# A streaming encoder step: one pool per tile tag, latent attention's tags laid anew, and reciprocal roots on ACT

## The chip, the cores and the metric

The kernel runs on one core of one Trainium2 chip. The metric is the device time of one execution in microseconds (us); of several runs the median counts.

## What is computed

Two layers of a hybrid encoder step, on a prompt of 512 rows (4 tiles of 128) and a sample of 8 streams with 16 new rows each and 1024 cached ones. All data are float32. Cut to what matters:

```
p = x @ w_in                     # columns for three branches
u = gelu(a_u);  v = layer_norm(gelu(a_v))          # per group of 64 columns
y_a = u * (w_s @ v + b_s)                          # branch A, chunked gMLP
q = rms(b_cq, g_cq) @ w_uq;  ckv = rms(b_ckv, g_ckv);  krope = rope(b_kr)
y_b = softmax(q_lat @ ckv.T + q_rope @ krope.T) @ ckv @ w_uv    # branch B, latent attention
y_c = stick_breaking(c_q, c_k, c_v)                # branch C
y = [rms(y_a) | rms(y_b) | rms(y_c)] * g_mix
x = layer_norm(ALPHA * x + y @ w_out)              # ln1
x = layer_norm(ALPHA * x + relu(x @ w_up + b_up)**2 @ w_down + b_down)   # ln2
rms(x) = x * rsqrt(mean(x*x) + EPS) * g;  layer_norm(x) = (x - mu) * rsqrt(var + EPS) * g + b
```

The normalised latents, keys and values of both lanes are outputs too.

## The kernel before

A float32 operand is split into a rounded part and a rest (`split`: a CAST on ACT, a subtraction on DVE or GpSimd, called POOL in the profile), and a product is three matmuls of these (`mm3`). Two lanes, prompt P and sample S, are written as generators and woven. Each layer runs in stages: `in` projects x (`xin` holds the transposed x, 32 KB a partition for the prompt and 8 KB for the sample), `mix` does the gMLP branch (`gm_group`, called for two prompt tiles at a time and for the sample rows), the stick-breaking of the prompt (`lane_psb`), and `latents`, whose results go to DRAM (`cqd`, `ckd`) and come back transposed; `mla` is the prompt's latent attention (`lane_pmla`), and `out` and `mlp` follow. The S lane works through the caches on the other side of the memory in the meantime.

Memory is a stack on each side. A stage opens a `pool_of`, whose tiles are told apart by tag, and closes it when it is done. After everything is written out, a planner (`Plan.schedule`, with a cost for every operation) sets the order of the instructions on each engine, and `follow` pins it. Its rule on memory and that of the framework are the same: a tile of a pool waits until all tiles of every closed pool whose region overlaps its own pool are done with. So a stage's first tile waits for the last one of the stage below it, wherever in the region it lies. Weights come through rings of raw buffers, `rawP` and `rawS` with three slots each, then as `w` (four slots); all DMAs are issued from the SP queue in the planned order.

Nearly every instruction is issued by one helper and so has line L417; DMAs have L433. Groups are therefore told apart by tile names: `gst` are the gMLP branch's sums and roots, `gvt` its gated values, `gh` their split form, `wsT` the spatial weights, `rs` the root of a norm, `mv` the mean and variance, `ss` a sum of squares, `wq`/`wuT` weights of latent attention, `cT`, `cN`, `kr` the split cached keys, values and rope keys, `sC`, `acc` and `x` banks of PSUM.

The root of a norm is made on POOL in two instructions, a multiply and add and a power of -0.5 (`rstd_of`), 70 times: 20 for `layer_norm`, 50 for `rms_to` and the latents. `gm_group` does the same six times on 128x4 or 128x8 numbers, and divides its mean on POOL too.

Of the kernel before, what the change touches and what calls it, by code (L numbers as in the profile page):

```python
# [11 lines left out]
F32 = mybir.dt.float32  # L12
# [3 lines left out]
ALU = mybir.AluOpType  # L16
# [482 lines left out]
def hybrid_step(  # L499
# [25 lines left out]
    def little(shape, dtype, tag):  # L525
        return sm.tile(shape, dtype, tag=tag + now["by"], name=tag, bufs=3 if now["by"] == "P" else 2)
# [20 lines left out]
    mhalf = cp.tile([128, 4, 4], F32, name="mhalf")  # L547
    dve.memset(mhalf, -0.5)
# [19 lines left out]

    class pool_of:


        def __init__(self, name, side=None):
            self.cm, self.side = tc.tile_pool(name=name, bufs=1, reuse_waits="tile", side=side), side

        def __enter__(self):
            self.slots = Slots(self.cm.__enter__(), pace, self.side)
            return self.slots

        def __exit__(self, *a):
            pace.plan.close_pool(self.slots.plan)  # L580
            return self.cm.__exit__(*a)
# [28 lines left out]

    def rstd_of(ss, k, n):
        t = little([128, 4], F32, "rs1")
        pool.tensor_scalar(t[:, :n], ss, k, EPS, ALU.mult, ALU.add)
        r = little([128, 4], F32, "rs2")
        pool.tensor_tensor(r[:, :n], t[:, :n], mhalf[:, 0, :n], ALU.pow)
        return r
# [112 lines left out]
    def gm_group(l, t0, nt, ws, gmx, gvt, pl, tag):  # L729
# [15 lines left out]
        pool.tensor_scalar(mu, mu, 1.0 / 64, 0.0, ALU.mult, ALU.add)  # L745
        dve.tensor_tensor(gv, gv, across(mu), ALU.subtract)
# [3 lines left out]
        pool.tensor_scalar(var, var, 1.0 / 64, EPS, ALU.mult, ALU.add)  # L750
        r = stat()
        pool.tensor_tensor(r, var, mhalf[:, :nt], ALU.pow)
# [271 lines left out]
    def lane_pmla(l):  # L1024
        mq_cm = pool_of(f"pmlb{l}", "left")
        mq = mq_cm.__enter__()
        mp_cm = pool_of(f"pmla{l}", "left")
        mp = mp_cm.__enter__()
# [195 lines left out]
        mq_cm.__exit__(None, None, None)  # L1224

    def lane_psb(l, zt, tt, yt_):
# [56 lines left out]
        def values(u):  # L1283
# [6 lines left out]
            for g in range(ng):  # L1290
                h = h0 + g
                for i in range(qt + 1):
                    b = slice((g * (qt + 1) + i) * 128, (g * (qt + 1) + i + 1) * 128)
                    pe.matmul(py[:, h * 128:(h + 1) * 128], wT[:, 0, b], vS[:, i, h].rearrange("p a d -> p (a d)"), start=(i == 0), stop=False)
                    pe.matmul(py[:, h * 128:h * 128 + 64], wT[:, 1, b], vS[:, i, h, 0], start=False, stop=(i == qt))
# [588 lines left out]
```

## Time and profile before

| | |
|---|---|
| three runs | 1797.98, 1798.75 and 1805.46 us, median 1798.75 |
| the profiled execution | 1802.48 us, of which the span of the trace is 1800.6 |
| busy over the span | PE 1689.7 (94%), DVE 1179.1 (65%), ACT 994.7 (55%), POOL 560.7 (31%) |
| mean granted clock of TensorE | 0.972 |
| DMA | 305.05 MB, 169 GB/s from and to HBM |

PE is TensorE's matmul, PEld its weight load. In a row of the timeline, the first number is the start in us from the span's start, the second the time until the group's end; the brackets give the idle time of the engine just before, and the instruction whose end released it. A clock of 1.00 is 2.4 GHz and 0.50 is 1.2 GHz.

### The profile page before, as it was taken

To read this page: it belongs to the slowest core of one execution; us is meant where nothing else is said; L and a number is where in the kernel's file an instruction comes from. 1 tells how busy PE (TensorE), PEld (TensorE's weight loads), DVE (VectorE), ACT (ScalarE), POOL (GpSimd) and SP (SyncE) were. 2 spreads that over 40 slices of the span, in tenths; PEclk is the share of its full clock that TensorE was granted. 3 is DMA by queue.
4 is the path that set the end of the run, shared out by engine and by line. 5 is a ranking of instruction groups with operands and counts; after the bars stand their busy time and mean duration, and the time that the engine had idled before them with its cause. 6 is when DMAs were issued, how large, how long until landed. Compare 5 with 4: busy or idle time off the path is not lost. (4 is left out here: it accounts for less than half of the span.)

```text
span 1800.6 us, 24422 instructions
## 1 busy us (share of the span) xinstructions
PE 1689.7 (94%) x8756; PEld 1421.8 (79%) x8756; DVE 1179.1 (65%) x1592; ACT 994.7 (55%) x1739; POOL 560.7 (31%) x478
## 2 busy tenths in 40 slices
PE   8997989899999999999899979899999989999998
PEld 6897878777877777888688968787877777788886
DVE  3575675865677577676726756858456774776666
ACT  4574684545665556463226737855457555564631
POOL 0122365743575300000101323666445643000001
PEclk9997999999999999999999979999999999999999
DMA  7225557346544688674442245663555355786732
GB/s 261 78 81 155 172 170 217 117 147 201 164 137 146 173 279 278 187 254 128 149 142 74 91 135 173 178 229 122 160 184 155 116 161 172 255 269 191 255 127 92
DMA packets 145817, 305.05 MB, mean 169 GB/s; under 512 B 32032, under 2 KB 46496, under 8 KB 145696
## 3 DMA queue, kind: packets, MB, share of 16 engines
q1 hardware_dynamic: 145696, 303.49, 53.1%
q8 instruction: 69, 1.13, 0.3%
q14 instruction: 52, 0.43, 0.1%
HBM read 286.14 MB, written 17.30 MB: 169 GB/s over the span
## 5 line engine op out<-in xcount | busy, mean ns | idle before, releaser
L417 PE MATMUL acc<-w,hT 128*128 128x512 f32 x1536 | 398.6, 397 | 3.0 <-DVE hT L417 1.4
L417 PE MATMUL acc<-yT,wx 128*128 128x512 f32 (+1 forms) x1632 | 400.0, 389 | 1.4 <-DVE wx L417 1.1
L417 PEld LDWEIGHTS acc<-yT,wx 128*128 128x128 f32 x1632 | 294.4, 193 | 59.5 <-DVE wx L417 1.5
L417 PEld LDWEIGHTS acc<-w,hT 128*128 128x128 f32 x1536 | 282.1, 189 | 65.9 <-DVE hT L417 3.1
L417 POOL TENSOR_TENSOR cT<-rawK,cT 128x512 fp32r<-128x512 f32 x128 | 201.1, 1578 | 178.7 <-ACT cT L417 157.1
L417 POOL TENSOR_TENSOR cN<-rawV,cN 128x512 fp32r<-128x512 f32 x128 | 194.3, 1524 | 167.7 <-ACT cN L417 160.9
L417 DVE TENSOR_TENSOR w<-rawP,w 128x1024 fp32r<-128x1024 f32 (+4 forms) x122 | 152.7, 1256 | 128.9 <-ACT w L417 127.8
L417 DVE TENSOR_TENSOR wS<-rawS,wS 128x1024 fp32r<-128x1024 f32 x144 | 175.2, 1223 | 78.9 <-ACT wS L417 78.7
L417 ACT CAST wS<-rawS 128x1024 fp32r<-128x1024 f32 x144 | 151.2, 1051 | 134.9 <-PE x L417 52.2
L417 PE MATMUL acc<-w,xT 128*128 128x512 f32 (+3 forms) x960 | 189.2, 352 | 4.0 <-ACT ev L417 2.2
L417 POOL TENSOR_SCALAR rs<-mv 128x1 f32<-128x1 f32 x20 | 24.3, 1216 | 528.7 <-DVE mv L417 528.5
L417 ACT CAST w<-rawP 128x1024 fp32r<-128x1024 f32 (+4 forms) x122 | 121.9, 1004 | 117.5 <-DMA rawP<-in_w_down_dram 61.5
L417 PEld LDWEIGHTS acc<-w,xT 128*128 128x128 f32 x960 | 161.1, 195 | 20.2 <-ACT ev L417 2.4
L417 DVE TENSOR_TENSOR xy<-xy,acc 128x512 f32<-128x512 f32 x128 | 86.8, 683 | 79.4 <-PE acc L417 78.4
L417 ACT CAST cN<-rawV 128x512 fp32r<-128x512 f32 x128 | 78.5, 619 | 76.1 <-DMA rawV<-in_t_ckvv_dram 35.9
L417 PE MATMUL x<-cN,pTs 128*128 128x256 f32 x512 | 98.7, 297 | 9.2 <-ACT cN L417 3.3
L417 PEld LDWEIGHTS x<-cN,pTs 128*128 128x128 f32 x512 | 82.1, 194 | 31.0 <-ACT cN L417 10.2
L417 PE MATMUL x<-wS,htS 128*128 128x512 f32 x384 | 100.7, 397 | 3.4 <-ACT wS L417 2.9
L417 ACT CAST cT<-rawK 128x512 fp32r<-128x512 f32 x128 | 78.5, 619 | 45.3 <-PE sC L417 20.1
L417 PE MATMUL sC<-wS,x1TS 128*128 128x512 f32 x384 | 98.4, 394 | 0.7 <-ACT x1TS L417 0.7
L417 DVE TENSOR_TENSOR wx<-rawP,wx 128x1024 fp32r<-128x1024 f32 x68 | 90.6, 1332 | 12.1 <-ACT wx L417 11.6
L417 PEld LDWEIGHTS x<-wS,htS 128*128 128x128 f32 x384 | 72.1, 189 | 21.1 <-ACT wS L417 3.3
(276 smaller groups left out, 2772.6 us busy)
## 6 DMA issues: line engine op xcount, KB each, us to landing
rawP<-in_t_wup_dram SPq DMA_DIRECT2D x64, 512.0 KB, 4.0
rawP<-in_w_down_dram SPq DMA_DIRECT2D x64, 512.0 KB, 4.1
rawS<-in_w_up_dram SPq DMA_DIRECT2D x64, 512.0 KB, 4.7
rawS<-in_w_down_dram SPq DMA_DIRECT2D x64, 512.0 KB, 4.4
rawK<-in_t_ckv_dram SPq DMA_DIRECT2D x64, 256.0 KB, 3.2
rawV<-in_t_ckvv_dram SPq DMA_DIRECT2D x64, 256.0 KB, 3.0
rawK<-in_t_sbk_dram SPq DMA_DIRECT2D x64, 256.0 KB, 2.8
rawV<-in_t_sbv_dram SPq DMA_DIRECT2D x64, 256.0 KB, 3.0
```

The costliest lines, as they stand in the source:

```text
L417: r = f(out, *a, **k)
```

## The change

Four edits.

1. `pool_of` no longer opens one pool for a stage, but one for each tag, when the tag is first used or where `lay` names it. When a stage is over, its tags are popped from the top of the side's stack as far as the stages above them are over too. Planner and framework thus wait for the region of a tag and no longer for that of a stage.
2. `lane_pmla` has one `pool_of` instead of two, and lays the tags of the first half of its work ahead in a fixed order.
3. `root` makes x^-0.5 on ACT, as exp(-0.5 ln(k x + EPS)): an ACTIVATE with Ln, whose scale is k and whose bias is a tile `eps`, and one with Exp. It takes the place of the two POOL instructions in `rstd_of` (70 times) and in `gm_group` (6 times). In `gm_group`, the mean's division on POOL and the subtraction on DVE become one `scalar_tensor_tensor` on DVE.
4. In the value product of `lane_psb`, the second matmul takes the same 128 columns as the first (80 matmuls of 64 columns before).

```diff
@@ pool_of
-        def __init__(self, name, side=None):
-            self.cm, self.side = tc.tile_pool(name=name, bufs=1, reuse_waits="tile", side=side), side
+        def __init__(self, name, side):
+            self.name, self.side, self.tags, self.over = name, side, {}, False
         def __enter__(self):
-            self.slots = Slots(self.cm.__enter__(), pace, self.side)
-            return self.slots
+            return self
+        def lay(self, *tags):
+            for tag in tags:
+                cm = tc.tile_pool(name=f"{self.name}_{tag}", bufs=1, reuse_waits="tile", side=self.side)
+                self.tags[tag] = Slots(cm.__enter__(), pace, self.side)
+                stacks[self.side].append((self, cm, self.tags[tag]))
+        def tile(self, shape, dtype, tag=None, name=None, bufs=1):
+            tag = tag or name
+            if tag not in self.tags:
+                self.lay(tag)
+            return self.tags[tag].tile(shape, dtype, tag, name, bufs)
         def __exit__(self, *a):
-            pace.plan.close_pool(self.slots.plan)
-            return self.cm.__exit__(*a)
+            self.over = True
+            st = stacks[self.side]
+            while st and st[-1][0].over:
+                _, cm, slots = st.pop()
+                pace.plan.close_pool(slots.plan)
+                cm.__exit__(*a)
...
+    def root(out, x, k):
+        act.activation(out, x, AF.Ln, bias=eps, scale=k)
+        act.activation(out, out, AF.Exp, scale=-0.5)
     def rstd_of(ss, k, n):
-        t = little([128, 4], F32, "rs1")
-        pool.tensor_scalar(t[:, :n], ss, k, EPS, ALU.mult, ALU.add)
-        r = little([128, 4], F32, "rs2")
-        pool.tensor_tensor(r[:, :n], t[:, :n], mhalf[:, 0, :n], ALU.pow)
+        r = little([128, 4], F32, "rs")
+        root(r[:, :n], ss, k)
         return r
@@ gm_group
-        pool.tensor_scalar(mu, mu, 1.0 / 64, 0.0, ALU.mult, ALU.add)
-        dve.tensor_tensor(gv, gv, across(mu), ALU.subtract)
+        dve.scalar_tensor_tensor(gv, across(mu), -1.0 / 64, gv, ALU.mult, ALU.add)
...
-        pool.tensor_scalar(var, var, 1.0 / 64, EPS, ALU.mult, ALU.add)
         r = stat()
-        pool.tensor_tensor(r, var, mhalf[:, :nt], ALU.pow)
+        root(r, var, 1.0 / 64)
@@ lane_pmla
-        mq_cm = pool_of(f"pmlb{l}", "left")
-        mq = mq_cm.__enter__()
         mp_cm = pool_of(f"pmla{l}", "left")
-        mp = mp_cm.__enter__()
+        mp = mq = mp_cm.__enter__()
+        mp.lay("cqT", "ckT", "d2", "qr", "rp2", "krT", "qT", "qrT", "rope", "mask", "knT", "vM")
@@ lane_psb
-                    pe.matmul(py[:, h * 128:h * 128 + 64], wT[:, 1, b], vS[:, i, h, 0], start=False, stop=(i == qt))
+                    pe.matmul(py[:, h * 128:(h + 1) * 128], wT[:, 1, b], vS[:, i, h].rearrange("p a d -> p (a d)"), start=False, stop=(i == qt))
```

The planner turns the first two edits into another order. Three places show it.

The first is ACT at the end of `mix` in layer 0, up to the split of the last two prompt tiles of the gMLP branch (the second `gh`); `gt<-gvt` is the square ahead of the variance, `junk` the sums of squares of norms. Before:

```order
L417 ACTIVATE gt<-gvt 128x512
L417 CAST w_1647<-rawP 128x768
L417 ACTIVATE junk,ss<-gt 128x256 x2
L417 ACTIVATE junk,ss<-acc 128x384
L417 CAST wq_1691<-rawS 128x768
L417 ACTIVATE junk,ss<-acc 128x256
L417 CAST wq_1696<-rawS 128x384
L417 ACTIVATE junk,ss<-acc 128x256
L417 CAST wq_1754<-rawS 128x768
L417 CAST wq_1759<-rawS 128x384
L417 CAST gh<-gvt 128x512
```

Now:

```order
L417 ACTIVATE gt<-gvt 128x512
L417 CAST w_1742<-rawP 128x768
L417 CAST mask<-rawP 128x128
L417 ACTIVATE gst<-gst,eps 128x8
L417 ACTIVATE gst<-gst 128x8
L417 ACTIVATE junk,ss<-gt 128x256
L417 CAST wq_1899<-rawS 128x384
L417 ACTIVATE rs<-ss,eps 128x1
L417 ACTIVATE junk,ss<-gt 128x256
L417 ACTIVATE rs<-rs 128x1
L417 CAST gh<-gvt 128x512
```

The root of `gst` is now two ACTIVATEs of ACT itself, three of the four `wq` CASTs stand ahead of it (two of them above these rows), and one between it and `gh`.

The second is the SP queue at the same place, where `cqd<-ev` writes latents to DRAM and `rawS<-in_w_uq` loads the weights of `wq`. Before:

```order
L433 DMA rawP<-in_c_mask_dram 128x128
L433 DMA cqd<-ev 128x384
L433 DMA rawP<-in_w_uq_dram 128x2x384
L433 DMA rope<-in_c_rope_dram 128x2x64
L433 DMA cq_1679<-cqd 128x384
L433 DMA rawS<-in_w_uq_dram 128x2x384
L433 DMA rawS<-in_w_uq_dram 128x384
L433 DMA rawP<-in_w_uq_dram 128x384
L433 DMA rawS<-in_w_uq_dram 128x2x384
L433 DMA rawP<-in_t_wkv_dram 128x1024
L433 DMA rawS<-in_w_uq_dram 128x384
L433 DMA rawS<-in_t_wukT_dram 128x1024
```

Now:

```order
L433 DMA rawS<-in_w_uq_dram 128x2x384
L433 DMA rawS<-in_w_uq_dram 128x384
L433 DMA rawS<-in_w_uq_dram 128x2x384
L433 DMA rope<-in_c_rope_dram 128x2x64
L433 DMA cq_1798<-cqd 128x384
L433 DMA cqd<-ev 128x384
L433 DMA rawP<-in_c_mask_dram 128x128
L433 DMA rawP<-in_w_uq_dram 128x2x384
L433 DMA rawP<-in_w_uq_dram 128x384
L433 DMA rawS<-in_w_uq_dram 128x384
L433 DMA rawP<-in_t_wkv_dram 128x1024
L433 DMA rawP<-cqd 128x768
```

Three of the loads of `wq` now stand ahead of the rope table and the mask; the transposed latents come back (`rawP<-cqd`) within these rows, which in the order of before they do twelve rows further on.

The third is DVE at the border between layer 0 and layer 1: the last norm of the prompt (`bst`, `mv`, `xy`), the weights of the next projection (`w`), and the transposed x of the next layer (`xT`). Before:

```order
L417 TENSOR_TENSOR xy<-xy,acc 128x512
L417 TENSOR_TENSOR w_8392<-rawP,w_8392 128x1024
L417 BN_STATS bst<-xy 128x6
L417 TENSOR_TENSOR w_8397<-rawP,w_8397 128x1024
L417 BN_AGGR mv<-bst 128x2
L417 TENSOR_TENSOR w_8402<-rawP,w_8402 128x1024
L417 SCALAR_TENSOR_TENSOR xy<-xy,mv,gl 128x1024
L417 TENSOR_TENSOR w_8407<-rawP,w_8407 128x1024
L417 SCALAR_TENSOR_TENSOR xy<-xy,rs_8328,gl 128x1024
L417 TENSOR_TENSOR xT<-acc,xT 128x4x128 x6
```

Now:

```order
L417 TENSOR_TENSOR xy<-xy,acc 128x512
L417 TENSOR_TENSOR w_8727<-rawP,w_8727 128x1024
L417 BN_STATS bst<-xy 128x6
L417 TENSOR_TENSOR xT<-acc,xT 128x4x128
L417 BN_AGGR mv<-bst 128x2
L417 TENSOR_TENSOR xT<-acc,xT 128x4x128
L417 SCALAR_TENSOR_TENSOR xy<-xy,mv,gl 128x1024
L417 TENSOR_TENSOR xT<-acc,xT 128x4x128
L417 SCALAR_TENSOR_TENSOR xy<-xy,rs,gl 128x1024
L417 TENSOR_TENSOR xT<-acc,xT 128x4x128 x3
L417 TENSOR_TENSOR w_8732<-rawP,w_8732 128x1024
L417 TENSOR_TENSOR w_8737<-rawP,w_8737 128x1024
```

The `xT` subtractions moved from behind four weight splits and the norm to between the norm's steps, behind one weight split.

## Rows read from the trace of the kernel before

**Rows 1.** The page's busy time: us, share of the span, instructions.

```profile
span 1800.6 us, 24422 instructions
...
PE 1689.7 (94%) x8756; PEld 1421.8 (79%) x8756; DVE 1179.1 (65%) x1592; ACT 994.7 (55%) x1739; POOL 560.7 (31%) x478
```

**Rows 2.** Stretches: length; busy and count of PE, PEld, DVE, ACT, POOL; clock; DMA share, GB/s.

```profile
136.00:180.00 44.00, 33.13 (x185) 31.83 (x184) 24.68 (x59) 19.14 (x49) 13.49 (x26) 0.77 0.50 155
...
256.00:276.00 20.00, 15.95 (x86) 12.49 (x86) 14.82 (x20) 14.81 (x31) 19.14 (x19) 0.83 0.69 165
...
880.00:910.00 30.00, 20.31 (x93) 16.60 (x91) 20.41 (x26) 8.07 (x13) 5.28 (x6) 0.83 0.53 160
...
1022.00:1080.00 58.00, 44.59 (x272) 42.01 (x271) 33.99 (x73) 23.59 (x58) 18.25 (x32) 0.82 0.45 137
```

**Rows 3.** The same view, of the stretches at the half clock.

```profile
142.00:152.24 10.24, 7.02 (x30) 7.02 (x31) 7.34 (x17) 3.25 (x7) 2.31 (x6) 0.50 0.34 113
...
169.31:179.55 10.24, 10.24 (x51) 10.24 (x51) 4.47 (x11) 4.23 (x9) 0.00 (x0) 0.50 0.26 72
...
892.94:903.18 10.24, 5.15 (x18) 4.59 (x19) 7.85 (x10) 4.56 (x8) 1.88 (x2) 0.50 0.80 204
...
1036.30:1049.95 13.65, 5.80 (x23) 5.62 (x24) 8.78 (x20) 4.14 (x10) 4.58 (x9) 0.50 0.36 123
...
1070.43:1077.26 6.83, 6.83 (x34) 6.83 (x33) 3.23 (x8) 2.35 (x6) 1.58 (x3) 0.50 0.43 145
```

**Rows 4.** Timeline, end of mix in layer 0, by engine; brackets: idle before, its releaser.

```profile
135.43 0.68 DVE L417 TENSOR_REDUCE gst<-gt 128x8 f32<-128x512 f32 x1
...
142.19 0.68 DVE L417 TENSOR_TENSOR gvt<-gvt,gst 128x512 f32<-128x512 f32 x1
...
139.43 1.65 POOL L417 TENSOR_TENSOR gst<-gst,mhalf 128x8 f32<-128x8 f32 x1
...
144.14 0.51 ACT L417 CAST wq<-rawS 128x384 fp32r<-128x384 f32 x1 [2.86 <-DMA rawS<-in_w_uq_dram]
144.56 0.61 ACT L417 CAST gh<-gvt 128x512 fp32r<-128x512 f32 x1
...
145.22 0.47 PE L417 MATMUL sC<-gh,wsT 128*128 128x128 f32 x1 [8.52 <-ACT gh L417]
```

**Rows 5.** Timeline of PE at the same place in layer 1.

```profile
1043.28 0.47 PE L417 MATMUL sC<-gh,wsT 128*128 128x128 f32 x1 [9.25 <-ACT gh L417]
```

**Rows 6.** Timeline at the border of the layers: ACT, DVE, PE.

```profile
893.88 1.04 ACT L417 CAST w<-rawP 128x1024 fp32r<-128x1024 f32 x1 [4.48 <-DMA rawP<-in_t_win_dram]
...
897.29 1.88 DVE L417 TENSOR_TENSOR xT<-acc,xT 128x512 fp32r<-128x512 f32 x3
...
898.03 2.18 PE L417 MATMUL acc<-identr,xy 128*128 128x128 f32 x9 [8.09 <-DVE xT L417]
```

**Rows 7.** Groups by shape: busy us, mean ns | idle before, releasers.

```profile
L417 POOL TENSOR_TENSOR rs<-rs,mhalf 128x1 f32<-128x1 f32 x70 | 46.6, 669 | 4.9 <-POOL rs L417 0.2
...
L417 POOL TENSOR_SCALAR rs<-mv 128x1 f32<-128x1 f32 x20 | 24.3, 1216 | 528.7 <-DVE mv L417 528.5
...
L417 ACT ACTIVATE xy<-acc,lr 128x128 f32<-128x128 f32 x32 | 11.9, 376 | 1.7 <-PE acc L417 1.2
...
L417 ACT ACTIVATION_READ_ACCUMULATOR p<-acc,m 128x1 f32 x32 | 6.4, 200 | 0.0
...
L417 PE MATMUL sC<-vS,wT 128*128 128x128 f32 x80 | 20.4, 302 | 0.0
...
L417 PE MATMUL sC<-vS,wT 128*128 128x64 f32 x80 | 18.3, 243 | 0.0
```

**Rows 8.** Timeline: POOL at two norms in latent attention, DVE at the end.

```profile
320.00 0.19 POOL L417 TENSOR_SCALAR rs<-mv 128x1 f32<-128x1 f32 x1 [1.61 <-DVE mv L417]
...
337.58 2.91 POOL L417 TENSOR_SCALAR rs<-mv 128x1 f32<-128x1 f32 x1 [2.32 <-DVE mv L417]
...
1795.62 1.28 DVE L417 SCALAR_TENSOR_TENSOR xy<-xy,rs,gl 128x1024 f32<-128x1024 f32 x1 [0.72 <-POOL rs L417]
```

More of the change, by code (lines that the diff above doesn't have):

```diff
@@ L545, in x_in @@
         return x_sample.rearrange("b s d -> (b s) d") if t == 0 else x_prompt[0, (t - 1) * 128:t * 128]
-    mhalf = cp.tile([128, 4, 4], F32, name="mhalf")
-    dve.memset(mhalf, -0.5)
+    eps = cp.tile([128, 1], F32, name="eps")
+    dve.memset(eps, EPS)
     xscr = drp.tile([128, 5, D], F32, name="xscr")
@@ L567, in at @@
         return max([pace.bank((id(ps), tag), BUFS[tag])] + [x if isinstance(x, float) else ready(x) for x in xs])
+    stacks = {"left": [], "right": []}
     class pool_of:
-        def __init__(self, name, side=None):
-            self.cm, self.side = tc.tile_pool(name=name, bufs=1, reuse_waits="tile", side=side), side
+        def __init__(self, name, side):
+            self.name, self.side, self.tags, self.over = name, side, {}, False
         def __enter__(self):
-            self.slots = Slots(self.cm.__enter__(), pace, self.side)
-            return self.slots
-        def __exit__(self, *a):
-            pace.plan.close_pool(self.slots.plan)
-            return self.cm.__exit__(*a)
+            return self
[9 more added lines that the diff above has]
+            return self.tags[tag].tile(shape, dtype, tag, name, bufs)
+        def __exit__(self, *a):
+            self.over = True
[4 more added lines that the diff above has]
+                cm.__exit__(*a)
     def tr(out, in_):
@@ L1223, in lane_pmla @@
         mp_cm.__exit__(None, None, None)
-        mq_cm.__exit__(None, None, None)
     def lane_psb(l, zt, tt, yt_):
```

## The prediction

> **What bounds the kernel now.** I read the busy times first: PE works 1689.7 of 1800.6 us, 94% of the span, and ACT 55%, POOL 31% [rows 1]. So PE sets the time, and only two things of it can be won: its idle time, 1800.6 - 1689.7 = 110.9 us, and what it loses where it runs at 1.2 instead of 2.4 GHz. Work taken off POOL is worth something only where PE waits for it in the end.
>
> Next come the stretches. Three of them stand out with a low busy share and a low clock together: the end of the gMLP branch and start of latent attention in layer 0 (136 to 180 us), the same in layer 1 (1022 to 1080), and the border of the layers (880 to 910). Their idle times are 44 - 33.1 = 10.9, 58 - 44.6 = 13.4 and 30 - 20.3 = 9.7 us [rows 2]. Inside them lie five stretches granted 0.50, in which PE is busy 7.0, 10.2, 5.2, 5.8 and 6.8 us, 35 us together [rows 3]; at full speed that work would take half, so the clock costs about 17.5 us. Idle time and clock make 34.0 + 17.5 = 51.5 us, a bound for what these places can give.
>
> Then the timeline of each place, for what ended last. In layer 0 PE stands 8.5 us ahead of the first product with `gh` [rows 4], in layer 1 9.25 us [rows 5], at the border 8.1 us for an `xT` subtraction on DVE [rows 6]. After the first and the third of these waits the clock is at the half level; before them it was full.
>
> **The first stall, followed back.** The sum for the variance is done at 135.43 + 0.68 = 136.1. POOL ends the power only at 139.43 + 1.65 = 141.1, since roots of other norms stand ahead of it. The multiplication on DVE starts 1.1 us later, behind weight splits, and ends at 142.9. ACT, however, makes `gh` only at 144.56, because it stood 2.86 us at a CAST of `wq` whose load had not landed [rows 4]. So two things hold PE up one after the other: the root's 5.0 us, and a load behind which ACT's queue stands. The change attacks both: the root goes to ACT, and the loads of `wq` are issued earlier, since `wq`'s tags need not wait for the whole of the stage on the same side.
>
> **The change part by part.**
>
> *The root on ACT.* No row of before shows an ACTIVATE on one column with a bias tile. The nearest ones are the accumulator's read on 128x1, 200 ns, and an ACTIVATE with a scale from memory on 128x128, 376 ns [rows 7]. A pair thus costs 0.4 to 0.75 us; I take 0.42, since one column is nearer to the first row. 76 pairs make 32 us more busy time on ACT (30 to 57), of an engine with 800 us to spare, and at least 46.6 + 24.3 = 70.9 us less on POOL by the two costliest groups [rows 7]. Beside this, the Trainium skill's page "ScalarE: Activation LUTs", What ACT_TABLE_LOAD costs, gives about 0.28 us for an ACTIVATE with a bias operand and 0.19 for one without, less 0.09 of overlap; by it, as an estimate, a pair would take 0.38 us and 76 pairs 29 us.
>
> *(a) The gMLP stall.* The floor: sum done at 136.1, root 0.4, DVE 0.7, ACT's `gh` 0.6, so 137.8; PE went idle at 136.70 (145.22 - 8.52), so 1.1 us would remain of 8.5. But the order of the changed kernel still has a CAST of `wq` between root and `gh` on ACT, the one whose load now stands last of the four, two sums of squares, and another root. I put 2.9 us for a load that is late again and 1 us for the rest on the floor: 5 us remain in each layer. That is -3.5 and -4.25, together -7.75. Ends: nothing, or -(7.4 + 8.1) = -15.5.
>
> *(b) The clock.* The 17.5 us come back only where the stalls that precede them go. About a third of the idle time of these places goes by (a), (c) and (d) below (15.75 of 34), so I take a third of the 17.5: -6. Ends: 0 and -17.5.
>
> *(c) The start of latent attention.* Beside the large stall PE idles 10.9 - 8.5 = 2.4 and 13.4 - 9.25 = 4.1 us there. The transposed latents come back twelve places earlier in SP's order. I take half, -3; ends 0 and -6.5.
>
> *(d) The border of the layers.* The DVE subtraction that PE waits for runs at 897.29, behind four weight splits, the last of which followed an ACT CAST that itself waited 4.48 us for its load [rows 6]. In the changed order the `xT` subtractions stand behind one weight split, between the steps of the norm, and ACT makes six `xT` CASTs ahead of its fourth weight. Three of these must still come behind a root. I let 3 of the 8.1 us remain: -5. Ends: 0 and -7. The root itself weighs little here: the POOL row at 337.58 takes 2.91 us for one number where the one at 320.00 takes 0.19 [rows 8], and the mean of the 20 is 1.22 [rows 7], so most of its length is not its own work. The Trainium skill's "SBUF — State Buffer", Who interferes with whom, says why it may be so: VectorE with two inputs in SBUF and a GpSimd instruction that reads SBUF lock each other out for the whole of an instruction. By that rule the root is late because DVE works, and a root taken off POOL would by itself win nothing at the border, where by the means of the rows it would win 1.22 + 0.67 - 0.42 = 1.5 us. The 5 us rest on DVE's and ACT's order and hold nothing for the root.
>
> *(e) Cached attention.* From 256 to 276 POOL is busy 19.1 of 20 us and PE idles 4.05 at a mean clock of 0.83 [rows 2]. Each root taken off POOL frees at least its power's 0.67 us there [rows 7]. I take -2 in layer 0 and -1 in layer 1; ends 0 and -7 (the idle time and as much of the clock).
>
> *(f) The end.* The last norm on DVE waits 0.72 us for POOL's root [rows 8]; ACT is idle then: -0.7.
>
> *(g) ACT's queue.* The roots add a wait. POOL stood 1.6 and 2.3 us for DVE's `mv` at the norms inside latent attention [rows 8]; now ACT, in order, stands there, and behind it the CASTs of `cT`, `cN` and `w`, for which PE and POOL wait. Together with the 32 us of work I take +3; ends 0 and +16 (the second rival).
>
> *(h) The wider matmul.* 80 matmuls go from 243 to 302 ns in the mean by the two rows that stand side by side [rows 7]: at most 80 x 0.059 = +4.7. Their durations overlap, and a weight load goes with each, so I take +1; the lower end is 0. The mean's division moves from POOL to DVE's next instruction, at no cost of its own: POOL's step falls out of a chain that (a) already counts.
>
> Sum: -7.75 - 6 - 3 - 5 - 3 - 0.7 + 3 + 1 = -21.5. The profiled execution took 1802.5, 3.7 above the median of the runs: 1802.5 - 21.5 - 3.7 = 1777.3 us.
>
> **The rivals.**
>
> *The waits come back under another name.* The loads of `wq` land no earlier in effect, since the raw ring has three slots and the fourth load still waits for one to be cast; ACT then stands at that CAST as before, and `gh` is as late as before. For it speaks that the 2.86 us wait was ended by the load and not by POOL, and that PE's products around `gh` hardly move; against it that three of four loads are ahead now. Then (a), (b) and (c) are nothing, (d) gives 2: -2 - 3 - 0.7 + 3 + 1 = -1.7, about 1797 us.
>
> *ACT becomes the queue that waits.* This is the one on the other side. Eight first norms of the prompt's tiles (four tiles, two layers) lie in latent attention's end, where ACT feeds `cT`, `cN` and the weights. If ACT stands 2 us (the mean of the 1.6 and 2.3 us that POOL stood) at each and PE has no cover, that is +16; on top of the first rival's sum of -1.7 less the +3 already in it, it gives 1798.75 - 4.7 + 16 = 1810 us. It decides from about 1.7 us a norm if the three stalls stay (14 over 8, past the bound for slower), and from over 4 us if they go as forecast. Against it: an order that puts the root behind enough other work on ACT would meet a finished `mv`.
>
> *More than forecast.* The stalls fall to their floors: (a) -15.5, (d) -7, (c) -5, and with them most of the half-clock time, -12; (e) -4, (f) -0.7, (g) and (h) +1: -43, about 1756 us. For it: the order of both engines at the border; against it: the CAST between root and `gh`.
>
> **How the numbers follow.** The forecast gets 0.57, more than forecast 0.16, the returned waits 0.15, ACT's queue 0.12. About 0.5% (9 us) is what a measurement of this kernel can tell from no change, so slower begins at 1807.7 and faster ends at 1789.8. Faster: 0.16 and all but 0.04 of the forecast's 0.57, with 0.02 of the returned waits: 0.71. Same: 0.13 + 0.04 = 0.17. Slower: 0.12. The range reaches over the returned waits and to just under the third rival's 1756, whose lower half is left out with ACT's queue, 0.2 together: 1753 to 1801.
>
> **What the changed profile would show.** (a) right: PE's wait for `gh` under 6 us in each layer, and ACT's wait for the load of `wq` gone or behind `gh`; wrong: PE's wait still over 8 us with ACT at a CAST of `wq` ahead of it. (b) right: fewer than 35 us of PE work at 0.50 in the three places, mean clock above 0.972. (c) less idle time from 150 to 180 beside the stall. (d) the wait for `xT` under 4 us; wrong if `xT` still starts behind the weights. (e) PE's waits for POOL's `kr`, `cN`, `cT` shorter. (g) wrong: ACT's ACTIVATE `rs<-mv` with idle time ahead of it, ended by DVE, and PE's waits for ACT's `cT`, `cN` or `w` grown by over 10 us. (f) no wait for a root ahead of the last norm over 0.3 us. The prediction is wrong as a whole if PE's idle time stays above 100 us at the same places.

## The result, and the profile after

The changed kernel takes 1741.54 us in the median of its runs (1738.5 to 1742.7); the kernel before, timed beside it, 1798.37 us. The ratio is 0.9684, with a 95% interval of 0.9638 to 0.973: 57 us less where 21.5 were forecast, and below the lower end of the range, 1753. The direction was right, the size was not. Two executions of all (one of `e_roots` below, one of the kernel before beside another run) had a granted clock of 0.84 instead of about 0.97 or more and are left out of medians and ratios.

The page of the changed kernel, beside [rows 1]:

```profile
span 1736.6 us, 24320 instructions
...
PE 1665.9 (96%) x8756; PEld 1404.2 (81%) x8756; DVE 1167.8 (67%) x1592; ACT 1017.5 (59%) x1891; POOL 461.8 (27%) x320
```

The span is 64 us shorter than that of the profiled execution of before. The medians differ by 57: the profiled execution of before is 4 us above its median, that of the changed kernel 3 below. 24 us of the 64 are PE busy time, for the same 8756 matmuls, and 40 are idle time. ACT is 23 us busier, POOL 99 us less.

To see where the time went, I cut both traces where PE has started the same amount of matmul work, each matmul counted at its spacing at full clock (about 230 ns for 512 columns, 146 for 320, 109 for 128 in both traces). Six of the stretches follow, in this order: the end of the gMLP branch with the first steps of latent attention in layer 0, the prompt's latent attention up to the first part of the MLP, the border of the layers, the first two again in layer 1, and the samples' attention of layer 1 beside the prompt's MLP. Each row has the length, then busy time and count of PE, PEld, DVE, ACT and POOL, then the clock, DMA share and GB/s. Before:

```profile
132.70:192.80 60.10, 49.23 (x322) 47.81 (x322) 35.08 (x81) 25.94 (x68) 13.49 (x26) 0.83 0.52 161
192.80:381.80 189.00, 172.17 (x1026) 147.67 (x1026) 139.95 (x217) 121.36 (x241) 108.15 (x82) 0.97 0.55 173
888.10:941.40 53.30, 43.01 (x229) 37.00 (x228) 20.75 (x25) 16.20 (x26) 2.52 (x2) 0.90 0.51 153
1025.40:1086.80 61.40, 47.98 (x313) 45.41 (x313) 34.90 (x79) 25.19 (x65) 17.15 (x30) 0.83 0.47 143
1086.80:1271.10 184.30, 173.43 (x1051) 151.42 (x1050) 136.58 (x226) 123.09 (x246) 107.25 (x83) 0.96 0.57 178
1271.10:1624.50 353.40, 336.74 (x1577) 270.93 (x1576) 229.74 (x255) 199.11 (x314) 126.35 (x85) 0.98 0.58 185
```

After:

```profile
133.80:180.40 46.60, 43.25 (x318) 41.47 (x317) 33.91 (x82) 29.73 (x92) 6.79 (x7) 0.96 0.62 187
180.40:360.50 180.10, 170.86 (x1031) 148.73 (x1030) 137.37 (x216) 121.81 (x253) 93.66 (x65) 0.97 0.57 182
867.30:914.50 47.20, 43.95 (x229) 36.40 (x228) 20.14 (x25) 16.77 (x28) 0.00 (x0) 0.93 0.56 174
996.90:1047.90 51.00, 44.74 (x312) 43.00 (x312) 37.19 (x83) 30.55 (x92) 6.49 (x7) 0.93 0.57 179
1047.90:1223.00 175.10, 167.14 (x1046) 146.71 (x1045) 133.74 (x217) 120.90 (x256) 96.79 (x65) 0.99 0.58 185
1223.00:1560.80 337.80, 329.88 (x1582) 267.14 (x1581) 229.51 (x259) 203.02 (x325) 121.95 (x78) 1.00 0.59 191
```

The two stretches around the gMLP branch go from 60.1 to 46.6 and from 61.4 to 51.0 us, together -23.9. Their idle time falls from 10.9 + 13.4 to 3.4 + 6.3 us, and their clock rises from 0.83 to 0.96 and 0.93, which takes 9.2 us from PE's busy time. Latent attention goes from 189.0 to 180.1 and from 184.3 to 175.1, together -18.1, of which 10.5 are idle time: one wait of 3.6 us for ACT's `cT`, and otherwise many of about 1 us. The border gives 6.1. The samples' attention of layer 1 gives 15.6, which no step of the prediction held.

The first stall in the timeline, beside [rows 4]; DVE's sum, ACT's two ACTIVATEs of the root, its last CAST of `wq`, the CAST of `gh`, and PE:

```profile
134.50 0.67 DVE L417 TENSOR_REDUCE gst<-gt 128x8 f32<-128x512 f32 x1
...
135.57 0.30 ACT L417 ACTIVATE gst<-gst,eps 128x8 f32<-128x8 f32 x1
135.90 0.21 ACT L417 ACTIVATE gst<-gst 128x8 f32<-128x8 f32 x1
...
136.92 0.51 ACT L417 CAST wq<-rawS 128x384 fp32r<-128x384 f32 x1 [0.41 <-DMA rawS<-in_w_uq_dram]
...
138.03 0.60 ACT L417 CAST gh<-gvt 128x512 fp32r<-128x512 f32 x1
...
138.68 0.33 PE L417 MATMUL sC<-gh,wsT 128*128 128x128 f32 x1 [1.16 <-ACT gh L417]
```

The root starts 0.4 us after DVE's sum ends and is made in 0.54 us. ACT waits 0.41 us for the load of `wq` where it waited 2.86. PE waits 1.16 us for `gh` where it waited 8.52, as good as the 1.1 us of the floor that the prediction had worked out and not taken. The way there is another one, though. From the end of DVE's sum to the end of `gh` it takes 3.46 us, where the floor had 1.7 (and the kernel before 9.1); but PE has matmuls for 2.35 us behind the sum, where it had them for 0.59.

The border of the layers, beside [rows 6], DVE and PE:

```profile
870.05 0.67 DVE L417 TENSOR_TENSOR xT<-acc,xT 128x512 fp32r<-128x512 f32 x1
...
870.78 1.57 PE L417 MATMUL acc<-identr,xy 128*128 128x128 f32 x8 [1.67 <-DVE xT L417]
873.25 1.12 PE L417 MATMUL acc<-identr,xy 128*128 128x128 f32 x4 [0.89 <-DVE xT L417]
875.04 3.35 PE L417 MATMUL acc<-w,xT 128*128 128x512 f32 x7 [0.68 <-DVE xT L417]
```

The wait for `xT` of 8.1 us has become three, of 1.67, 0.89 and 0.68 us.

The roots on ACT by their groups:

```profile
L417 ACT ACTIVATE rs<-ss,eps 128x1 f32<-128x1 f32 x50 | 14.9, 298 | 0.3
L417 ACT ACTIVATE rs<-rs 128x1 f32<-128x1 f32 x70 | 14.1, 202 | 0.7
...
L417 ACT ACTIVATE rs<-mv,eps 128x1 f32<-128x1 f32 x20 | 5.9, 297 | 54.9 <-DVE mv L417 54.9
```

The two instructions take 0.30 and 0.20 us. The 20 roots of the full norms wait 54.9 us for DVE's `mv`: ACT does stand there, as the rival said. What that costs is the question of one experiment below.

### The profile page after: what moved, and what is told of

Same layout as the page of the kernel before. It is cut to its first block, busy times and chain, and to the rows that moved or that the text cites. A ratio compares the mean times of both kernels' runs of the same rounds, so it can differ in the third digit from the quotient of the medians.

```text
span 1736.6 us, 24320 instructions
## 1 busy us (share of the span) xinstructions
PE 1665.9 (96%) x8756; PEld 1404.2 (81%) x8756; DVE 1167.8 (67%) x1592; ACT 1017.5 (59%) x1891; POOL 461.8 (27%) x320
## 4 chain that ended last, share of the span: by engine, by line
PE 73%; ACT 8%; DVE 7%; DMA 7%; issue 4%; POOL 2%; SPq 0%; ACTq 0%; POOLq 0%; DVEq 0%
PE acc L417 52%; PE sC L417 11%; PE x L417 10%; DVE xy L417 2%; POOL cN L417 1%; DMA rawV<-in_t_ckvv_dram 1%; DMA rawK<-in_t_sbk_dram 1%; ACT w L417 1%; POOL cT L417 1%; DVE w L417 1%; ACT cN L417 1%; ACT cT L417 1%; DMA rawS<-in_w_up_dram 1%; DVE a L417 1%; DMA rawP<-in_w_down_dram 0%
## 5 line engine op out<-in xcount | busy, mean ns | idle before, releaser
L417 PEld LDWEIGHTS acc<-yT,wx 128*128 128x128 f32 x1632 | 291.8, 191 | 61.4 <-issue 3.9
L417 DVE TENSOR_TENSOR w<-rawP,w 128x1024 fp32r<-128x1024 f32 (+4 forms) x122 | 149.0, 1227 | 111.6 <-ACT w L417 110.0
L417 PEld LDWEIGHTS acc<-w,xT 128*128 128x128 f32 x960 | 159.8, 193 | 20.5 <-ACT w L417 1.5
L417 PE MATMUL x<-cN,pTs 128*128 128x256 f32 x512 | 92.4, 290 | 11.5 <-ACT cN L417 5.8
L417 PEld LDWEIGHTS x<-cN,pTs 128*128 128x128 f32 x512 | 77.7, 190 | 30.3 <-ACT cN L417 11.8
L417 DVE TENSOR_TENSOR wx<-rawP,wx 128x1024 fp32r<-128x1024 f32 x68 | 85.9, 1265 | 12.6 <-ACT wx L417 11.9
L417 PEld LDWEIGHTS sC<-wS,x1TS 128*128 128x128 f32 x384 | 71.8, 188 | 16.5 <-DVE wS L417 0.5
```

What stands on the lines that cost most here:

```text
L417: r = f(out, *a, **k)
```

## The experiments

After the result I had theory A: the gMLP stall has two causes in a row, the late loads of `wq` and the late root, each of which hides the other; the pools take away the first, the roots the second, and the border belongs to the pools. Its rivals: B, the roots alone are the gain; C, the parts' gains simply add. A fourth, D, came with the 15.6 us that nobody had forecast: the planner makes another order of everything with each edit, and part of a gain is only the luck of an order.

### The parts alone

`e_pools`, the changed kernel with these lines back (and, with them, the mean's division on POOL and the narrow second matmul):

```diff
-        root(r[:, :n], ss, k)
...
+        pool.tensor_scalar(t[:, :n], ss, k, EPS, ALU.mult, ALU.add)
...
+        pool.tensor_tensor(r[:, :n], t[:, :n], mhalf[:, 0, :n], ALU.pow)
...
+        pool.tensor_scalar(var, var, 1.0 / 64, EPS, ALU.mult, ALU.add)
...
-        root(r, var, 1.0 / 64)
+        pool.tensor_tensor(r, var, mhalf[:, :nt], ALU.pow)
```

> The changed kernel with all roots and the gMLP mean back on GpSimd and the narrow second matmul: the pools and the layout alone. Theory A (the gMLP stall has two causes in a row, the late weights of wq and the late root, and the pools take away the first only): PE still waits 5 to 6 us for gh in each layer, the border of the layers is as in the changed kernel; about 1770 us, ratio to before 0.98 to 0.99. Theory B (the roots are the gain): 1790 us or more, ratio above 0.993. Theory C (the edits' gains simply add): its gain and that of the roots alone sum to the whole 57 us.

Measured: 1762.0 us, ratio 0.9794 (0.9764 to 0.9824). POOL, ACT and PE at the stall of layer 0:

```profile
139.56 0.90 POOL L417 TENSOR_SCALAR rs<-ss 128x1 f32<-128x1 f32 x1
...
141.18 1.64 POOL L417 TENSOR_TENSOR gst<-gst,mhalf 128x8 f32<-128x8 f32 x1
...
142.97 0.51 ACT L417 CAST wq<-rawS 128x384 fp32r<-128x384 f32 x1 [2.01 <-DMA rawS<-in_w_uq_dram]
...
145.82 0.61 ACT L417 CAST gh<-gvt 128x512 fp32r<-128x512 f32 x1
...
146.48 0.47 PE L417 MATMUL sC<-gh,wsT 128*128 128x128 f32 x1 [9.74 <-ACT gh L417]
```

Three of the four loads of `wq` are ahead in SP's order here as in the changed kernel (the fourth is issued at 139.1 us, there at 134.0, before at 140.9), and still PE waits 9.7 us, no less than before, where theory A had 5 to 6. On POOL two roots of other norms stand ahead of the power of `gst`; ACT's CAST of `wq` is late again, and its CAST of `gh` stands behind `wuT`. So the earlier loads alone buy nothing at this stall. The same stretches as above, first and second of each layer:

```profile
132.80:191.50 58.70, 45.53 (x319) 43.68 (x318) 35.05 (x84) 26.57 (x70) 20.31 (x30) 0.85 0.51 157
191.50:370.10 178.60, 167.76 (x1031) 146.15 (x1030) 133.91 (x215) 118.59 (x235) 104.47 (x79) 0.99 0.58 182
1008.70:1065.00 56.30, 44.81 (x312) 43.09 (x312) 37.10 (x83) 25.76 (x66) 24.72 (x33) 0.88 0.52 164
1065.00:1245.10 180.10, 170.12 (x1048) 148.73 (x1047) 136.09 (x220) 121.28 (x244) 104.49 (x81) 0.98 0.58 179
```

The gMLP stretches stay at 58.7 and 56.3 us; latent attention falls to 178.6 and 180.1. That is where the pools' gain lies, beside the border. Theory B, with 1790 us or more, is out.

`e_roots`, the kernel before with edit 3 alone (`rstd_of` and `gm_group` as in the diff of the change):

> The kernel before with the roots and the gMLP mean off GpSimd, nothing else: stage pools stay. Theory A: ACT still stands at the cast of wq ahead of gh, PE's waits for gh stay above 6 us, the border's xT wait stays at about 8 us; gain of 5 to 10 us, ratio 0.994 to 0.997. Theory B: gain above 30 us, ratio below 0.983.

Measured: 1766.7 us, ratio 0.9814 (0.9773 to 0.9855); theory A had 0.994 to 0.997 and is wrong here, and theory B's number comes out, though `e_pools` has refuted B. At the stall of layer 0, ACT and PE:

```profile
135.20 0.21 ACT L417 ACTIVATE gst<-gst 128x8 f32<-128x8 f32 x1
...
136.45 0.60 ACT L417 CAST gh<-gvt 128x512 fp32r<-128x512 f32 x1
...
137.81 0.23 PE L417 MATMUL sC<-gh,wsT 128*128 128x128 f32 x1
```

Not only is the root made earlier: ACT's CAST of `gh` stands ahead of three of the four CASTs of `wq`, although their loads are as late in SP's order as before. As I read the two orders, the planner has `gh` ready early with the root on ACT itself and puts it ahead; the wait for the load, which I had taken for a second cause, was one only because the late root let the CASTs get ahead of `gh`. The gMLP stretches fall to 50.1 and 48.8 us, and latent attention hardly moves, with 184.7 and 185.6:

```profile
134.30:184.40 50.10, 46.24 (x319) 44.28 (x318) 32.96 (x80) 29.60 (x91) 2.43 (x4) 0.90 0.52 159
184.40:369.10 184.70, 171.47 (x1030) 147.77 (x1029) 136.22 (x217) 124.14 (x257) 97.31 (x68) 0.97 0.58 181
1009.20:1058.00 48.80, 42.34 (x313) 39.88 (x311) 35.50 (x82) 29.35 (x91) 2.46 (x4) 1.00 0.58 180
1058.00:1243.60 185.60, 173.33 (x1048) 150.48 (x1048) 137.03 (x220) 123.74 (x259) 96.61 (x66) 0.96 0.57 178
```

The border's wait stays, as expected:

```profile
884.34 2.82 PE L417 MATMUL acc<-identr,xy 128*128 128x128 f32 x12 [7.74 <-DVE xT L417]
```

### Halves of the roots

`e_gmpool` (only the six roots and means of the gMLP branch back on POOL) and `e_normpool` (only the 70 of the norms back), each from the changed kernel, in this order:

```diff
+        pool.tensor_scalar(var, var, 1.0 / 64, EPS, ALU.mult, ALU.add)
...
-        root(r, var, 1.0 / 64)
+        pool.tensor_tensor(r, var, mhalf[:, :nt], ALU.pow)
```

> The changed kernel with only the six roots and means of the gMLP branch back on GpSimd. Theory A: the wait for gh comes back to about 5 us in each layer and brings a stretch of half clock with it, +10 to +16 us, about 1755 us. Rival (the order after it hides it, or most of the gain lies outside the gMLP branch): within 5 us of the changed kernel, about 1742 us.

```diff
-        root(r[:, :n], ss, k)
...
+        pool.tensor_scalar(t[:, :n], ss, k, EPS, ALU.mult, ALU.add)
...
+        pool.tensor_tensor(r[:, :n], t[:, :n], mhalf[:, 0, :n], ALU.pow)
```

> The changed kernel with the 70 roots of the norms back on GpSimd, those of the gMLP branch on ACT. Theory A: only GpSimd's busy stretches in attention and the last norm lose, +2 to +6 us, about 1746 us. Rival (the gain of about 18 us in the samples' attention of layer 1, which was not forecast, comes from GpSimd's relief): +15 us or more, 1757 us.

Measured: 1751.65 us (ratio 0.9737, 0.9708 to 0.9767) and 1751.66 us (0.974, 0.971 to 0.977), 10 us more than the changed kernel each. For the first this is the low end of theory A's number by another way: PE's wait for `gh` did not come back (4.0 us in four pieces). POOL has nothing else to do there now and starts on the root at once:

```profile
134.68 2.10 POOL L417 TENSOR_SCALAR gst<-gst 128x8 f32<-128x8 f32 x1 [5.03 <-DVE gst L417]
136.87 1.75 POOL L417 TENSOR_TENSOR gst<-gst,mhalf 128x8 f32<-128x8 f32 x1
```

The root is done 4.1 us after DVE's sum, and PE still waits only 1.29 us there, since it has matmuls in the meantime. With the norms' roots back instead, PE waits 5.8 us for `gh`, and the two gMLP stretches are nearly as long as before (59.0 and 57.2 us). For `e_normpool` theory A had 2 to 6 us, and its rival is out too, for the samples' attention of layer 1 stays short, at 336.8 us. So the place is slow with the norms' roots in POOL's queue, and not with the root of `gst` alone in it (46.6 us by length in the changed kernel, 45.1 with that root on POOL, in layer 0; 51.0 and 54.7 in layer 1). The +10 us of both are within what another order does to a time, as the next group shows, so I don't divide them further.

### The order alone

Three kernels differ from the one before, and two from the changed one, only in a number of the planner's costs, by 3% to 13% of that number. `b_p1` and `a_p1`:

```diff
-        return 0.19 + n * 0.00084 + 0.19 * accum + 0.06 * (len(ins) > 1)
+        return 0.2 + n * 0.00084 + 0.19 * accum + 0.06 * (len(ins) > 1)
```

`b_p2`, `a_p2`:

```diff
-        return 0.145 + n * slope
+        return 0.15 + n * slope
```

`b_p3`:

```diff
-        return max(n * 0.000435 + 0.008, 0.111)
+        return max(n * 0.000435 + 0.009, 0.111)
```

> The kernel before with one number of the planner's costs changed (an ACT instruction's fixed part 0.20 us instead of 0.19), which changes nothing but the order on all engines. Theory D (part of the gain, the 18 us in the samples' attention of layer 1, is only what another order happens to give): 1775 to 1790 us, with that stretch as short as in the changed kernel. Rival (orders differ little): within 5 us of 1798.4 us.

> The kernel before with another number of the planner's costs changed (a VectorE instruction's fixed part 0.15 us instead of 0.145). As for the one with ACT's number: theory D expects times that scatter by 10 us or more among such orders, its rival within 5 us of 1798.4 us. The waits for gh and xT stay in both.

> The kernel before with a third of the planner's numbers changed (a wide matmul's fixed part 0.009 us instead of 0.008): another order, nothing else. Theory D: between 1775 and 1798 us like the other two; the loss at the end of the gMLP branch stays as it is in all orders of the kernel before, and the stretch of the samples' attention in layer 1 is shorter.

> The changed kernel with the planner's number for an ACT instruction's fixed part at 0.20 us instead of 0.19: another order, nothing else. Theory D (orders of one kernel scatter by some 10 to 20 us, and the changed kernel's own order is a lucky one of its kind): 1745 to 1765 us. Rival (the changed kernel is as fast in any order): within 5 us of 1741.5 us.

> The changed kernel with the planner's number for a VectorE instruction's fixed part at 0.15 us instead of 0.145: another order, nothing else. Theory D: 1745 to 1765 us. Rival: within 5 us of 1741.5 us.

| kernel | median us | ratio to before | 95% interval |
|---|---|---|---|
| `b_p1` | 1784.88 | 0.9936 | 0.9911 to 0.9961 |
| `b_p2` | 1775.54 | 0.9873 | 0.9846 to 0.9901 |
| `b_p3` | 1806.73 | 1.0018 | 1.0 to 1.0037 |
| `a_p1` | 1739.01 | 0.9648 | 0.9631 to 0.9665 |
| `a_p2` | 1748.59 | 0.9702 | 0.9686 to 0.9718 |

Theory D is right for the kernel before: by their ratios its orders scatter over 26 us, and its own order is one of the slow ones (`b_p3` is as slow, where 1775 to 1798 us were expected). It is wrong for the changed kernel, whose own order is no lucky one: there are 10 us between its three, with its own in the middle. `a_p2` is within theory D's range in time, but by its ratio only 3 us above the changed kernel.

The wait for `gh`, which I expected to stay in `b_p1` and `b_p2`, did so in `b_p1` (15.5 us). In `b_p2`, with every root on POOL, it fell from 17.8 to 4.9 us by the order alone:

```profile
PE sC L417 <- ACT gh L417: 4.9, 2, 2.4
```

Yet its gMLP stretches are hardly shorter, 57.4 and 61.0 us where they were 60.1 and 61.4. PE waits for the RMS-normed latents (`ev`, 3.9 us) and the queries (`qn`, 3.8 us) there instead. So the one long wait that the prediction priced is not what makes this place long.

The samples' attention of layer 1, 353.4 us before and 337.8 after, in two of the other orders of the kernel before:

```profile
1275.20:1615.40 340.20, 332.59 (x1577) 269.03 (x1576) 233.96 (x255) 200.04 (x315) 128.42 (x85) 0.99 0.60 190
```

```profile
1256.20:1598.60 342.40, 331.87 (x1580) 267.36 (x1579) 230.78 (x258) 200.11 (x318) 127.81 (x85) 1.00 0.60 190
```

13.2 and 11.0 of the 15.6 us are to be had without the change. Averaged over the orders, the kernel before has a ratio of 0.9957 (four orders) and the changed one 0.9678 (three): 0.0279 x 1798 = 50 us belong to the change, and about 7 of the 57 to the two orders that were compared. Four orders are few: the spread of their ratios makes their mean uncertain by some 6 us, as an estimate (standard deviation 0.0066, over the root of four).

The parts in two more orders each (`r_` from `e_roots`, `p_` from `e_pools`, with the same two numbers changed):

> The kernel before with the roots alone on ACT (as in e_roots), in another order (the planner's number for an ACT instruction's fixed part at 0.20 us). If the roots' gain of 32 us is theirs and not their order's: 1760 to 1775 us, PE's waits for gh short, the wait of about 8 us for xT at the border of the layers still there. If it was the order's luck: 1780 us or more.

> The roots alone on ACT, in a third order (a VectorE instruction's fixed part at 0.15 us). As for the second order: 1760 to 1775 us if the gain belongs to the roots, 1780 us or more if to the order.

> The pools and the layout alone (as in e_pools), in another order (ACT's number). If the gain of 36 us is the pools': 1755 to 1772 us, PE's wait for gh still 5 us or more in at least one layer, the wait for xT at the border under 3 us. If it was the order's: 1780 us or more.

> The pools and the layout alone, in a third order (VectorE's number). As for the second order: 1755 to 1772 us if the gain belongs to the pools, 1780 us or more if to the order.

| kernel | median us | ratio to before | 95% interval |
|---|---|---|---|
| `r_p1` | 1765.9 | 0.9809 | 0.975 to 0.9869 |
| `r_p2` | 1761.4 | 0.9765 | 0.9702 to 0.9828 |
| `p_p1` | 1753.23 | 0.9734 | 0.9684 to 0.9784 |
| `p_p2` | 1754.41 | 0.9743 | 0.9693 to 0.9793 |

Both gains belong to their parts; the pools' orders are even 1 to 2 us below the range expected. The wait for `gh` was a worse sign than I expected, as in `b_p2`: in `p_p2` it is 3.1 us in all, and the gMLP stretches are still 57.6 and 56.6 us. There PE waits a little later, for a rope product of the queries on ACT and for latents that come back from DRAM:

```profile
163.12 0.75 PE L417 MATMUL sC<-identr,qd 128*128 128x128 f32 x4 [2.16 <-ACT qd L417]
167.25 1.09 PE L417 MATMUL acc<-identr,rawP 128*128 128x128 f32 x4 [3.39 <-DMA rawP<-ckd]
```

The latents pass a norm before they go to DRAM. That they come late because its root stands in POOL's queue fits that `e_normpool`, with only the norms' roots back, has the long stretches again, and waits of 3.4 us for `ev` and 3.2 us for `ckd`. The path through the latents is argued from that and not shown by a run of its own: waits for `ckd` of the same size occur with all roots on ACT too (below).

The next table gives the loss of each stretch: its length less PE's work in it, which is the same in all (per layer 40 and 160 us in the first two rows, then 40 and 320, and 1614 in the whole span), averaged over the orders of a kind. Each trace is one execution: those of the changed kernel and of `e_narrow` below, which have the very same order, differ by 5 us in the first stretch and by 9 in the span.

| us lost | before, 4 orders | roots alone, 3 | pools alone, 3 | both, 3 |
|---|---|---|---|---|
| gMLP and start of latent attention, both layers | 40.3 | 21.1 | 33.8 | 17.8 |
| latent attention of the prompt, both layers | 53.8 | 50.0 | 36.9 | 34.2 |
| border of the layers | 13.2 | 11.2 | 5.3 | 7.5 |
| samples' attention, layer 1 | 25.0 | 26.8 | 17.5 | 20.5 |
| the whole span less PE's work | 179.0 | 152.8 | 140.5 | 123.9 |
| mean ratio to before | 0.9957 | 0.9796 | 0.9757 | 0.9678 |

The roots take 19 us out of the first row, the pools 17 out of the second and 8 out of the third. From 0.9957, the roots alone give 29 us, the pools alone 36, both 50. That is 15 less than their sum, but the four orders of before alone spread by 0.0145, 26 us, so whether the gains overlap (theory C) stays open; row by row the first two nearly add (19.2 + 6.5 against 22.5, and 3.8 + 16.9 against 19.6).

### The layout, the width, and ACT's queue

`e_oldlay`, the changed kernel without edit 2:

```diff
-        mp = mq = mp_cm.__enter__()
-        mp.lay("cqT", "ckT", "d2", "qr", "rp2", "krT", "qT", "qrT", "rope", "mask", "knT", "vM")
+        mq_cm = pool_of(f"pmlb{l}", "left")
+        mq = mq_cm.__enter__()
+        mp_cm = pool_of(f"pmla{l}", "left")
+        mp = mp_cm.__enter__()
```

> The changed kernel without edit 2: latent attention has its two pools of before, no tags laid ahead (one pool per tag stays). Theory A (the tags' own waits do the work, and the layout adds the early start of latent attention): +3 to +8 us, 1745 to 1750 us. Rival (the layout adds nothing): within 3 us of 1741.5 us.

Measured: 1760.17 us, ratio 0.979 (0.9759 to 0.9822), 19 us more than the changed kernel, where its own orders differ by 10; theory A had 3 to 8 us, the rival less than 3. It is one order only. The two stretches of latent attention take 184.2 and 182.7 us in it, near the 184.7 and 185.6 of the roots alone, and the border is as short as in the changed kernel. PE in layer 0 at the transposes of the latents that come back from DRAM (`rawP`), with old layout:

```profile
162.70 1.08 PE L417 MATMUL acc<-identr,rawP 128*128 128x128 f32 x4 [3.46 <-DMA rawP<-ckd]
```

in the changed kernel, and in `e_narrow`, which has the layout and the order of the changed kernel:

```profile
156.72 0.63 PE L417 MATMUL acc<-identr,rawP 128*128 128x128 f32 x4
```

```profile
161.32 1.09 PE L417 MATMUL acc<-identr,rawP 128*128 128x128 f32 x4 [2.79 <-DMA rawP<-ckd]
```

PE waits 3.46 us for `ckd` with the old layout and not at all in the trace of the changed kernel, but `e_narrow` waits 2.79 us at the same place, so this wait comes and goes between executions of one order and says nothing of the layout; the lengths of the stretches do, as the end of this section shows.

`e_narrow`, the changed kernel with the second matmul of 64 columns, in the very same order:

```diff
-    pe.matmul(py[:, h * 128:(h + 1) * 128], wT[:, 1, b], vS[:, i, h].rearrange("p a d -> p (a d)"), start=False, stop=(i == qt))
+    pe.matmul(py[:, h * 128:h * 128 + 64], wT[:, 1, b], vS[:, i, h, 0], start=False, stop=(i == qt))
```

> The changed kernel with the second matmul of the values narrow again (64 columns); every engine's order is that of the changed kernel. The prediction took +1 us for the wider one, with 0 and +4.7 as ends: so this kernel within 1 us of 1741.5 us, at the lowest 1737. Rival (the width costs nothing, since the weight load sets the pace): no difference at all.

Measured: 1742.29 us, ratio 0.9682 (0.9653 to 0.9712) against 0.9684: the width costs nothing that can be measured.

`e_double`, the changed kernel with a second, unread root behind each:

```diff
...
+        act.activation(d, x, AF.Ln, bias=eps, scale=k)
+        act.activation(d, d, AF.Exp, scale=-0.5)
```

> The changed kernel with each of the 76 roots made twice on ACT, the second time into a tile that nobody reads (152 more ACTIVATEs, some 35 us of busy time; the order moves a little with it). The prediction's term for ACT's queue, +3 us for such an amount of work: 1742 to 1750 us with the scatter of orders. Rival (ACT is the queue that PE waits for): +16 us or more, above 1757 us, with PE's waits for ACT grown.

Measured: 1744.83 us, ratio 0.9683 (0.9662 to 0.9704). The two costliest groups that it adds:

```profile
L417 ACT ACTIVATE spare<-ss,eps 128x1 f32<-128x1 f32 x50 | 14.4, 287 | 0.0
L417 ACT ACTIVATE spare<-spare 128x1 f32<-128x1 f32 x70 | 14.1, 201 | 0.0
```

152 more ACTIVATEs, 37 us by the groups of its trace, cost nothing beyond the scatter. This prices ACT's work and not its standing at `mv`, since the second pair never waits (0.0 us idle before it). For the standing the two traces of before and after are enough: PE's waits for ACT's `cT`, `cN` and `w` were 21.1 us and are 19.2, where the rival had them grow by more than 10. So the rival of ACT's queue is out, and the 54.9 us are idle time that ACT has.

With all 18 traces side by side, cut at the same work, each of the three places goes with one part of the change (lengths in us, both layers together in the first two rows):

| stretch | with the part | without it |
|---|---|---|
| gMLP and start of latent attention; part: the norms' roots on ACT | 96 to 106 (10 traces) | 112 to 122 (8) |
| latent attention of the prompt; part: the layout, edit 2 | 352 to 362 (10) | 367 to 379 (8) |
| border of the layers; part: one pool per tag, edit 1 | 45 to 48 (11) | 51 to 55 (7) |

The ranges do not overlap; they are 6, 5 and 3 us apart at the nearest, so a single trace near an edge proves little, and the kinds prove more. `e_gmpool` is on the short side of the first row with the root of `gst` on POOL, and `e_normpool` on the long side with it on ACT. `e_oldlay`, with one pool per tag and the old layout, is on the short side of the third row and on the long one of the second. In the samples' attention of layer 1 the kinds overlap (337 to 353 us).

## Why the prediction was wrong

Two steps failed most. The sum has no term for what the layout does inside the prompt's latent attention, and the runs showed 17 us there. And (a) takes the length of the gMLP place from one named wait and its next cause, where the runs showed that the norms' roots in POOL's queue make it long, whichever wait PE stands at: with (b) and (c), 23.9 us in the two traces and 22.5 over the orders.

**(a) The gMLP stall: the wrong price, and its match with the floor is luck.** The step is "I put 2.9 us for a load that is late again and 1 us for the rest on the floor". ACT waited 0.41 us for that load, and PE's waits fell to 1.16 us in layer 0 and 1.03 + 1.15 in layer 1. But the chain from the sum to `gh` was 1.8 us longer than that of the floor, and PE had work for 1.8 us longer; the two cancel. I had read two waits in a row off one timeline and priced them as if each would stay when the other went. With the root early, `gh` goes ahead of the load's CAST (`e_roots`); with the loads early and the root late the whole wait stays (`e_pools`). And the wait itself can go without a gain: in `b_p2` and `p_p2` it is 4.9 and 3.1 us, and the stretches stay long.

**(b) The clock: right, but for a slip.** 15.75 of 34 us are 46% and not "about a third"; by its own rule the term would have been -8.1 and not -6. PE's busy time fell by 9.2 us in the two gMLP stretches and rose by 0.9 at the border, 8.3 us less in the three places.

**(c) The start of latent attention: nothing.** Forecast -3. Beside the waits for `gh`, PE idled 2.4 and 3.3 us in the two gMLP stretches before, and 2.2 and 4.1 now.

**(e) Cached attention: right for what it priced.** Forecast -3 for roots that leave POOL. PE's waits for POOL in the two stretches of latent attention fell from 6.4 to 1.1 us with the roots alone (`e_roots`), and over the orders the roots alone took 3.8 us out of these stretches.

**The layout: the largest miss.** Edit 2 stood in the sum only as the early start, in (c). The two stretches lost 18.1 us, and over the orders of each kind 17 us with the pools alone; with all traces side by side that goes with the layout. I looked for what a removed wait would give only where one long wait showed; here it was spread over many of about 1 us. That loads and latents come earlier throughout because the tags are laid ahead is my reading of it, and no run shows the path.

**(d) The border: right.** Forecast -5, measured 53.3 - 47.2 = 6.1 us in the stretch and 5.7 over the orders; three waits of 3.2 us together where 3 us were left over. With the roots alone the wait is 7.7 us instead of 8.1 (`e_roots`), so nothing for the root was about right.

**(f) The end: right.** DVE's last step of the norm no longer waits for a root; 0.1 us between the two, where 0.72 were:

```profile
1729.92 1.29 DVE L417 SCALAR_TENSOR_TENSOR xy<-xy,mv,gl 128x1024 f32<-128x1024 f32 x1
1731.31 1.28 DVE L417 SCALAR_TENSOR_TENSOR xy<-xy,rs,gl 128x1024 f32<-128x1024 f32 x1
```

**(g) ACT's queue, +3: nothing** (`e_double`). ACT does stand at `mv` as forecast; the other half of that sign, PE's waits for ACT grown by over 10 us, did not come. **(h) The wider matmul, +1: nothing** (`e_narrow`).

**What else was not in the sum.** About 7 of the 57 us are the luck of the two orders, and the 15.6 us in the samples' attention of layer 1 are mostly of that kind: over the orders they are 4.5. I had argued from one trace as if its losses were the kernel's, when a third of those in the samples' attention of layer 1 belonged to that order alone.

**The rivals.** "More than forecast" came nearest (the named waits fall to their floors), and its 1756 us was still too high: of the 18 us in latent attention it held 4, and it had nothing for the orders. "The waits come back" happened only in kernels that keep the norms' roots on POOL, and not in all of them. "ACT becomes the queue that waits" is refuted. The low end of the range stood on the third rival; it should have taken in the bounds of (b), (c) and (e) as well, and the scatter of the orders.

## What to carry to other kernels

Two waits in a row in one timeline need not be two causes: ask which of them ordered the queue in which the other stands, and give the floor, not a sum of both, a fair chance. Nor is the longest wait the price of its place: in `b_p2` it went, and the place stayed as long. Where a scheduler rewrites the order with every edit, change a number that means nothing and time the kernel before in three or four orders first; differences below that scatter (26 us of 1798 here) can't be put down to an edit, and the loss that all orders share is what a change can win for sure. A small instruction on a third engine may cost by its place in that engine's queue more than by its length: the gMLP branch's own root, 3.9 us on an otherwise empty POOL, did not lengthen its place beyond the scatter, and the 70 roots of the norms did.

## What the runs showed of the hardware

An ACTIVATE on one column took 0.30 us with a bias tile and 0.20 without, back to back 0.54 us for a pair on 128x8, whose second starts 0.03 us after the first has ended. The Trainium skill's "ScalarE: Activation LUTs", What ACT_TABLE_LOAD costs, gives 0.28 and 0.19 us, and the trace agrees to 0.02 us. On POOL, the root of `gst` with an otherwise empty queue still took 2.10 + 1.75 us in `e_gmpool`, seven times as long as the pair's 0.54, which I had not expected with nothing ahead of it. The 2.10 us are not the instruction's own length alone: in the kernel before, the multiply and add on 128x8 took 0.43 us in the mean of eight. What made it longer is not shown by a run.
